# Four gate pairs on seven products, a weave that begins with the key groups, and a new order of the up groups

## The chip, the cores and the metric

The kernel runs on one core of one Trainium2 chip. The metric is the device time of one execution in microseconds (us), and the number that counts is the median of several runs.

## The reference

One layer of a streaming encoder: a feed-forward block, a mixer, a second feed-forward block and a gated input embedding, with a layer norm behind each of the first three. 256 tokens, 2048 channels, all in float32. The change lies in the mixer, whose input `x` is the output of the first norm:

```python
proj = x @ w_in
mq, mk, mv, mo, mi, mf, sq, sk, sv, ga, gb = _split_cols(proj)
qk = jax.nn.silu(_causal_conv(jnp.concatenate([mq, mk], axis=-1), conv_w))
...
h = _mlstm_chunkwise(q, k, v, log_i, log_f)          # 4 heads of 256: the memory half
y_m = head_norm(h) * jax.nn.sigmoid(mo)
y_sb = _stick_breaking(sq, sk, sv)                   # 8 heads of 128: the stick half
merged = jax.nn.sigmoid(ga) * (y_m @ w_up_m) + jax.nn.sigmoid(gb) * (y_sb @ w_up_sb)
return merged @ w_out
```

`ga` and `gb` are 2048 columns each. All other matrix products of the layer have the same form, 256 rows times a weight that is read once from memory.

## The kernel before

**Products of split halves.** A float32 product is made of three faster products. Activations and weights are each split into a rounded high half and the rest as a low half, and TensorE multiplies high by high, high by low and low by high (lines 1462 to 1464) into one PSUM bank. Activations are split once. Each page of a weight (256 rows of 512 columns, 512 KB) is split when it is due: ScalarE casts the high half (line 1388) and VectorE subtracts it to get the low half (line 1392). A `Unit` is the work of one page for one half of the tokens: six matmuls of 512 columns.

**Two ways to do a pair of column groups.** The plain way, `group` (line 410), takes each page for both token halves. So 2048 rows times two groups of 512 columns are 16 pages, 16 splits and 32 units. The other way, `seven` (line 423, called by `both7`), treats the pair as a 2 by 2 block product and forms seven products in place of eight: 28 units for the same pair. It needs sums of weight pages, and each of its 28 units needs a split of its own. Of the sums, some are made by VectorE (line 443) and some by a second load that adds in memory, issued on GpSimd's queue (line 449). `loaded` says which: where it is `every`, two of the four sums of each quad are loads and two are VectorE's. It also needs sums of the activations (`x1T.forms`), made by `forms_later` (line 394): for each of four chunks VectorE does two additions (line 399), four half-width operations (lines 382 to 386) and two subtractions (line 359). When the seven products are there, `both7`'s `done` and `rest` combine them with five VectorE operations and three copies on ScalarE.

**Order.** The whole order of work is written by this program, in one pass. `program` lists units. `weave(main, side)` spreads the side list evenly through the main list. For each unit the pass emits six matmuls, then runs the generators of `Sched` that are due (a clock of 1.297 us per full unit), then emits splits ahead of use until six split pages are held, and then loads ahead of the splits until six (`mix`) or ten (`woven`) unsplit pages are held (`HELD`, line 32). Each engine works through its own queue in that order, so a weight's split stands in VectorE's queue behind every operation that the generators emitted before it. Loads go out on SP's queue in that order too, between the stores of the norm's result, `put_away` (line 331). Such a store waits for an addition that GpSimd's queue issued (line 625), which waits for VectorE's multiplication (line 621).

**The mixer before.** It begins with the plain groups q0, gates, q1, k0 and k1 (lines 1103 to 1107; `conv` at line 868 follows each q or k group with two times six VectorE operations, line 889, behind PE's transposes, line 874). `forms_later` is started after q1. Then comes the weave. Its main list is v0, v1, four stick groups `sb` (the last half as wide), the two plain groups of the first gate pair, `branch(0, 0)` and `branch(0, 1)`, and `ups(0)`, `ups(1)`, `ups(2)`, each a memory half (`w_up_m`, needs `ymT`) followed by a stick half (`w_up_sb`, needs `ysbT`). Its side list is five sevens: stick values, output gates, and gate pairs 1, 2 and 3. After it come `ups(3)` and the output groups. Generators beside it do the four mLSTM heads (`mlstm`, `gated`) and the eight stick heads (`stick`, in lanes). Both chunks of `ymT` (line 1046) are stored to memory when they are ready and brought back before `ups(0)`.

Of the kernel before, what the change touches and what calls it, by code (L numbers as in the profile page):

```python
# [211 lines left out]
        self.name = name  # L212


def weave(main, side):

    n = sum(u.cols for u in main if isinstance(u, Unit))
    out, at, seen = [], 0, 0
    for u in main:
        out.append(u)  # L220
        if isinstance(u, Unit):
            seen += u.cols
            while at < len(side) and at * n < seen * len(side):
                out.append(side[at])
                at += 1
    return out


def flat(pairs):
    return [u for p in pairs for u in p]  # L230
# [7 lines left out]
def kernel(  # L238
# [39 lines left out]
    def big(shape=(P, 1024)):  # L278
        return page_pool.tile(list(shape), F32, name="big", tag="page")
# [114 lines left out]
    def forms_later(act, c):  # L394

        act.whole[c] = big()
        for t in range(TT):
            hi, lo = (act.tiles[c, t][:, k].rearrange("q k s -> q (k s)") for k in range(2))
            nc.vector.tensor_tensor(out=act.whole[c][:, t * COL:(t + 1) * COL], in0=hi, in1=lo, op=ALU.add)
        yield 4.0  # L400
        yield from form_turn(act, c)
# [8 lines left out]
    def group(w, rows, col0, cols, act, done, seed=None):  # L410

        accs = [{} for _ in range(TT)]
        pairs = []
        for i, r in enumerate(rows):
            tile = plain(rows_of(w, r, col0, cols))
            pairs.append([Unit(tile, t, accs[t], act, r // COL, r % COL // P,
                               i == 0, i == len(rows) - 1, done) for t in range(TT)])
            for u in pairs[-1]:
                u.onto = seed is not None
                u.seed = seed if i == 0 else None  # L420
        return pairs
# [436 lines left out]
    def qk_done(which, g):  # L858
        stage = {}

        def done(ps, t):
            stage[t] = temp()
            nc.scalar.copy(stage[t][:], ps)
            if t == TT - 1:
                sched.spawn(conv(which, g, stage), DELAY["cv0"])
        return done
# [85 lines left out]
    def bring_ym_back(units):  # L952

        def one(c, t):
            ymT.tiles[c, t] = act_tile()
            nc.sync.dma_start(out=ymT.tiles[c, t][:].bitcast(F32), in_=ym_rows(c, t))

        out = []
        for i in range(0, len(units), 4):
            out += [lambda i=i: one(i // 8, i // 4 % 2)] + units[i:i + 4] if i < 16 else units[i:i + 4]  # L960
        return out

    def mlstm(h):
        yield from wait("gates", ("qk", 0, h), ("qk", 1, h), ("v", 0, h // 2), ("v", 1, h // 2))
# [55 lines left out]
    def gated(h):  # L1020

        yield from wait(("hs", h), ("mo", 0, h // 2), ("mo", 1, h // 2))
        due = max(sched.now, st.get("gated", 0.0))
        st["gated"] = due + GATED_GAP
        yield due - sched.now
        hs = st["hs", h // 2][:, h % 2]
        for t in range(TT):
            nc.vector.tensor_tensor(out=hs[:, t], in0=hs[:, t], in1=st["mo", t][:, h * DM:(h + 1) * DM], op=ALU.mult)
        yield bank(DELAY["m4"])
        ps = misc([P, TT, 2, P])  # L1030
        parts = []
        for t in range(TT):
            for b in range(2):
                nc.tensor.transpose(ps[:, t, b], hs[:, t, b * P:(b + 1) * P], ident[:])
                k = 2 * (h % 2) + b
                parts.append((ymT.get(h // 2, t)[:, :, k], ps[:, t, b], hs[:, t, b * P:(b + 1) * P],
                              st["cw"][:, 64 + 2 * h + b:65 + 2 * h + b]))
        for _, src, y, g in parts:
            activate(y, src, ACT.Copy, scale=g)
        for d, _, y, _ in parts:  # L1040
            nc.scalar.copy(d[:, 0], y)
            nc.vector.tensor_tensor(out=d[:, 1], in0=y, in1=d[:, 0], op=ALU.subtract)
        for t in range(TT):
            ymT.mark(h // 2, t, 2)
            if ymT.ready(h // 2, t):
                sched.spawn(put_ym_away(h // 2, t), DELAY["away"])

    def stick(h):
# [50 lines left out]
    def in_sequence(gens):  # L1099
        for g in gens:  # L1100
            yield from g
# [1 line left out]
    head = group(w_in, range(0, D, 2 * P), 0, COL, x1T, qk_done(0, 0))  # L1103
    program.extend(skewed(head[:SKEW]) + flat(head[SKEW:]))
    program.extend(flat(group(w_in, range(0, D, 2 * P), 4096, 2 * HM + 2 * DS, x1T, gates_done)))
    for which, g in ((0, 1), (1, 0), (1, 1)):
        program.extend(flat(group(w_in, range(0, D, 2 * P), which * 1024 + g * COL, COL, x1T, qk_done(which, g))))
        if which == 0:
            program.append(lambda: [sched.spawn(forms_later(x1T, c), 4.0 + 12.0 * c) for c in range(4)])
    program.append(lambda: [sched.spawn(in_sequence([mlstm(a), mlstm(a + 1)])) for a in (0, 2)])  # L1110

    def v(g):
        return flat(group(w_in, range(0, D, 2 * P), 2048 + g * COL, COL, x1T, v_done(g)))
# [16 lines left out]
    ga0 = sq0 + 3 * HS * DS  # L1130
    gt = {}

    def gate_done(g, half):
        def done(ps, t):
            if (g, t) not in gt:
                gt[g, t] = big()
            activate(gt[g, t][:, half * COL:(half + 1) * COL], ps, ACT.Sigmoid)
            flags.add(("gate", g, t, half))
        return done

    def merged(g, t):
        return gt[g // 2 * 2, t][:, g % 2 * COL:(g % 2 + 1) * COL]

# [15 lines left out]
            yield 3.0  # L1159
            yield from form_turn(mergedT, g)  # L1160

    def branch(g, half):
        return flat(group(w_in, range(0, D, 2 * P), ga0 + half * D + g * COL, COL, x1T, gate_done(g, half)))

    def ups(g, swap=False):
        parts = [flat(group(w_up_m, range(0, HM * DM, 2 * P), g * COL, COL, ymT, up_done(g, 0, swap))),
                 flat(group(w_up_sb, range(0, HS * DS, 2 * P), g * COL, COL, ysbT, up_done(g, 1, not swap)))]
        if swap:
            parts.reverse()
        return parts[0] + parts[1]  # L1170

    every = (range(4), range(4))

# [9 lines left out]
    def pair(g):  # L1183
        return both7(w_in, ga0 + g * COL, ga0 + D + g * COL, x1T, gate_dest(g), in_two(lambda t: gt[g, t], lambda k, t: ("gate", g, t, k)), every)

    program.append(lambda: [sched.spawn(lane()) for _ in range(2)])
    program.append(lambda: sched.spawn(in_sequence([gated(h) for h in range(HM)])))
    gate = branch(0, 1)
    main = v(0) + v(1) + sb(*SB_GROUPS[0]) + sb(*SB_GROUPS[1]) + [Mode("wide")] + sb(*SB_GROUPS[2]) + sb(*SB_GROUPS[3]) + [lambda: sched.spawn(lane())] + branch(0, 0) + gate[:4] + bring_ym_back(gate[4:] + ups(0)) + ups(1) + ups(2)
    mode("woven")  # L1190
    program.extend(weave(main, in_line([both7(w_in, sq0 + 2 * HS * DS, sq0 + 2 * HS * DS + COL, x1T, sv_dest, sv_ready, later),
                                   both7(w_in, 3072, 3072 + COL, x1T, mo_dest, mo_ready, every), pair(1), pair(2), pair(3)])))
    mode("mix")
    program.append(bring_back)
    program.append(lambda: [sched.spawn(merge_turn(g, t), 1.0 + 2.0 * g + t) for g in range(3) for t in range(TT)])
# [60 lines left out]
    third, fourth = out_group(2), out_group(3)  # L1256
    side = in_line([out7(0, 1)])
    mode("out")
    main = ups(3)
    program.extend(main[:10] + side[:1] + main[10:])  # L1260
    woven = weave(flat(third + fourth[:-SKEW]), side[1:])
    program.extend(woven[:20])
# [257 lines left out]
```

## Time and profile before

| | us |
|---|---|
| median of the three runs | 2152.23 |
| the three runs | 2152.07, 2153.82, 2152.23 |
| the profiled execution | 2151.87 |
| its span, first to last instruction | 2150.2 |

The time of an execution is about 1.7 us more than the span, which lies around it. PE stands for TensorE's matmuls, PEld for its weight loads, DVE for VectorE, ACT for ScalarE, POOL for GpSimd, SP for the queue that issues most transfers. Matmuls are pipelined, so that their recorded durations overlap, and a PE that is busy all the time says little. What tells is the distance from the start of one matmul to the start of the next. The same holds in a small way for VectorE: its operations begin a little before the recorded end of the one before, and the pitch from start to start is what one costs in a full queue. In the mixer the q0 group starts near 688 us, q1 near 725, k0 near 748, k1 near 771, the weave near 794, and `ups(3)` near 1250.

### The profile page before, as it was taken

The page shows a single profiled execution, that of the slowest core. Times are in us where ns is not written, and L with a number is a line of the kernel's source. Part 1 is how long each engine was busy: PE and PEld are TensorE (multiplying, and loading weights), DVE is VectorE, ACT ScalarE, POOL GpSimd, SP SyncE. Part 2 cuts the span into 40 slices and gives each one's busy share as a digit, 9 for nine tenths or more (in the row PEclk, how much of TensorE's full clock was granted, in tenths as well). Part 3 has the DMA queues.
Part 4 walks back from the last instruction along what each step waited for, and adds up shares of the span by engine and source line. Part 5 has one row for each costly group of instructions (what it writes and reads, how often), then busy time and mean ns, then how long its engine had stood idle before and what let it go on. Part 6 is the DMA issues. An engine that isn't in the chain of part 4 may idle for free.

```text
span 2150.2 us, 27845 instructions
## 1 busy us (share of the span) xinstructions
PE 2141.2 (100%) x9742; PEld 1775.6 (83%) x9742; DVE 1866.3 (87%) x2003; ACT 1499.6 (70%) x1946; POOL 160.9 (7%) x190
## 2 busy tenths in 40 slices
PE   9999999999999999999999999999999999999999
PEld 7888888888888888888888887888888888888887
DVE  7899999899987798878888999799998998999773
ACT  6676777777777665678876667757676776776872
POOL 0011000011000000000000000011000011000000
PEclk9999999999999999999999999999999999999999
DMA  9799788998894676868898888788878998889562
GB/s 363 232 264 268 246 262 248 277 266 274 260 313 152 215 263 200 253 208 217 263 280 265 270 234 288 235 224 264 259 248 250 273 280 265 258 261 288 214 181 110
DMA packets 151964, 537.02 MB, mean 250 GB/s; under 512 B 17168, under 2 KB 21776, under 8 KB 151824
## 3 DMA queue, kind: packets, MB, share of 16 engines
q1 hardware_dynamic: 125616, 439.82, 57.1%
q0 software_dynamic: 26208, 95.43, 23.9%
q8 instruction: 76, 1.25, 0.2%
q14 instruction: 64, 0.52, 0.1%
HBM read 528.90 MB, written 6.29 MB: 249 GB/s over the span
## 4 chain that ended last, share of the span: by engine, by line
PE 96%; DVE 2%; DMA 1%; issue 0%; ACT 0%; SPq 0%; DVEq 0%; ACTq 0%
PE mm L1462 31%; PE mm L1464 31%; PE mm L1463 31%; PE ms L363 2%; DVE split L1392 1%; DVE temp L889 0%; DMA raw<-in_ffn_w_dram 0%; DVE raw L443 0%; DMA raw<-in_w_out_dram 0%; PE ms L1086 0%; PE ms L978 0%; PE ms L1056 0%; PE ms L993 0%; ACT split L1388 0%; DVE actT L359 0%
## 5 line engine op out<-in xcount | busy, mean ns | idle before, releaser
L1392 DVE TENSOR_TENSOR split<-raw,split 128x1024 fp32r<-128x1024 f32 (+1 forms) x1102 | 1296.7, 1212 | 158.1 <-ACT split L1388 145.2
L1388 ACT CAST split<-raw 128x1024 fp32r<-128x1024 f32 (+1 forms) x1102 | 1109.2, 1043 | 356.4 <-DVE raw L443 124.9
L1462 PE MATMUL mm<-split,actT 128*128 128x512 f32 x3056 | 1198.4, 392 | 2.1 <-ACT mm L295 2.0
L1464 PE MATMUL mm<-split,actT 128*128 128x512 f32 x3056 | 1185.3, 388 | 0.0
L1463 PE MATMUL mm<-split,actT 128*128 128x512 f32 x3056 | 1184.3, 388 | 0.5 <-DVE split L1392 0.5
L1464 PEld LDWEIGHTS mm<-split,actT 128*128 128x128 f32 x3056 | 574.1, 188 | 118.5 <-DVE actT L359 0.4
L1462 PEld LDWEIGHTS mm<-split,actT 128*128 128x128 f32 x3056 | 574.5, 188 | 116.5 <-ACT mm L295 2.4
L1463 PEld LDWEIGHTS mm<-split,actT 128*128 128x128 f32 x3056 | 574.8, 188 | 114.4 <-DVE split L1392 2.1
L443 DVE TENSOR_TENSOR raw<-raw 128x1024 f32<-128x1024 f32 x214 | 261.3, 1222 | 2.3
L449 POOL DMA_DIRECT2D raw<-in_ffn_w_dram x124 | 108.9, 997 | 1028.6 <-DVE split L1392 859.4
L359 DVE TENSOR_TENSOR actT<-temp,actT 128x512 fp32r<-128x512 f32 (+1 forms) x94 | 62.7, 683 | 47.4 <-ACT actT L358 47.4
L295 ACT ACTIVATE temp<-mm 128x512 f32<-128x512 f32 (+1 forms) x54 | 31.2, 582 | 76.1 <-PE mm L1464 75.8
L717 ACT COPY big<-mm 128x512 f32<-128x512 f32 x80 | 46.8, 585 | 30.4 <-PE mm L1464 30.2
L358 ACT CAST actT<-temp 128x512 fp32r<-128x512 f32 (+1 forms) x94 | 56.9, 616 | 13.0 <-DVE temp L383 7.1
L449 POOL DMA_DIRECT2D raw<-in_w_in_dram x38 | 33.3, 988 | 407.7 <-DVE split L1392 394.9
L724 ACT COPY mm<-big 128x512 f32<-128x512 f32 x96 | 56.4, 590 | 0.0
L371 ACT COPY temp<-ms 128x512 f32<-128x512 f32 x44 | 25.8, 587 | 41.6 <-PE ms L363 40.9
L661 DVE TENSOR_TENSOR temp<-mm,temp 128x512 f32<-128x512 f32 x72 | 49.7, 690 | 5.0 <-PE mm L1464 3.8
L625 POOL DMA_DIRECT2D big<-in_ln_b_dram x12 | 10.4, 864 | 353.1 <-DVE big L621 219.6
L1308 DVE TENSOR_TENSOR temp<-temp,big 128x512 f32<-128x512 f32 (+1 forms) x10 | 5.8, 585 | 32.5 <-ACT temp L295 32.5
L291 ACT ACT_TABLE_LOAD x26 | 33.4, 1283 | 0.5
L359 DVE TENSOR_TENSOR actT<-big,actT 128x512 fp32r<-128x512 f32 x24 | 16.5, 689 | 12.1 <-ACT actT L358 12.1
(140 smaller groups left out, 637.7 us busy)
## 6 DMA issues: line engine op xcount, KB each, us to landing
raw<-in_ffn_w_dram SPq DMA_DIRECT2D x528, 512.0 KB, 6.4
raw<-in_w_in_dram SPq DMA_DIRECT2D x168, 512.0 KB, 5.6
raw<-in_ffn_w_dram POOLq DMA_DIRECT2D x124, 512.0 KB, 8.7
raw<-in_w_in_dram POOLq DMA_DIRECT2D x38, 512.0 KB, 8.9
raw<-in_w_out_dram SPq DMA_DIRECT2D x32, 512.0 KB, 4.7
raw<-in_w_ple_gate_dram SPq DMA_DIRECT2D x32, 512.0 KB, 4.8
raw<-in_w_up_m_dram SPq DMA_DIRECT2D x16, 512.0 KB, 6.2
raw<-in_w_up_sb_dram SPq DMA_DIRECT2D x16, 512.0 KB, 4.8
```

Of the source, the lines that this page charges most:

```text
L358: nc.scalar.copy(hi, ps)
L359: nc.vector.tensor_tensor(out=lo, in0=ps, in1=hi, op=ALU.subtract)
L443: nc.vector.tensor_tensor(out=out.tile[:, :, :cols], in0=a.tile[:, :, :cols], in1=b.tile[:, :, :cols], op=ALU.add)
L449: nc.gpsimd.dma_start(out=whole(out.tile[:]), in_=whole(src), accum_op=ALU.add)
L661: nc.vector.tensor_tensor(out=out, in0=a, in1=b, op=op)
L717: nc.scalar.copy(xres(t, g * COL), ps)
L724: nc.scalar.copy(ps, xres(t, g * COL))
L1388: nc.scalar.copy(hi[:, ks], r[:, ks])
L1392: nc.vector.tensor_tensor(out=lo[:, ks], in0=r[:, ks], in1=hi[:, ks], op=ALU.subtract)
L1462: nc.tensor.matmul(ps, hi, w[0][:, k, :u.cols], start=first, stop=False, skip_group_check=u.onto)
L1463: nc.tensor.matmul(ps, hi, w[1][:, k, :u.cols], start=False, stop=False, skip_group_check=u.onto)
L1464: nc.tensor.matmul(ps, lo, w[0][:, k, :u.cols], start=False, stop=last, skip_group_check=u.onto)
```

## The change

All four gate pairs go through `both7`, so `branch` and `gate_done` are gone and the side list has six sevens. The k groups and v groups move into the weave's main list, in a new order. `weave` gets a lead of 8 full units: nine units of the side follow the first unit of the main list, one follows each unit after that, and the last eight units of the main list have none beside them. `forms_later` starts one group earlier, with delays of 1, 13, 25 and 37 in place of 4, 16, 28 and 40. mLSTM heads 0 and 1 run first, then 2 and 3, so only the first chunk of `ymT` is stored and brought back, now around the last stick group. Of the up groups 0 to 2 all three memory halves come first, then all three stick halves.

```diff
-def weave(main, side):
+def weave(main, side, lead=0):
...
-    out, at, seen = [], 0, 0
+    out, at, seen = [], 0, lead * COL
...
-        out = []
-        for i in range(0, len(units), 4):
-            out += [lambda i=i: one(i // 8, i // 4 % 2)] + units[i:i + 4] if i < 16 else units[i:i + 4]
-        return out
+        return [lambda: one(0, 0)] + units[:4] + [lambda: one(0, 1)] + units[4:]
...
-            if ymT.ready(h // 2, t):
+            if h < 2 and ymT.ready(h // 2, t):
...
-    for which, g in ((0, 1), (1, 0), (1, 1)):
-        program.extend(flat(group(w_in, range(0, D, 2 * P), which * 1024 + g * COL, COL, x1T, qk_done(which, g))))
-        if which == 0:
-            program.append(lambda: [sched.spawn(forms_later(x1T, c), 4.0 + 12.0 * c) for c in range(4)])
-    program.append(lambda: [sched.spawn(in_sequence([mlstm(a), mlstm(a + 1)])) for a in (0, 2)])
+    def qk(which, g):
+        return flat(group(w_in, range(0, D, 2 * P), which * 1024 + g * COL, COL, x1T, qk_done(which, g)))
+
+    program.append(lambda: [sched.spawn(forms_later(x1T, c), 1.0 + 12.0 * c) for c in range(4)])
+    program.extend(qk(0, 1))
...
-    def branch(g, half):
-        return flat(group(w_in, range(0, D, 2 * P), ga0 + half * D + g * COL, COL, x1T, gate_done(g, half)))
-
-    def ups(g, swap=False):
...
+    def up_m(g):
+        return flat(group(w_up_m, range(0, HM * DM, 2 * P), g * COL, COL, ymT, up_done(g, 0, False)))
+
+    def up_sb(g):
+        return flat(group(w_up_sb, range(0, HS * DS, 2 * P), g * COL, COL, ysbT, up_done(g, 1, True)))
...
+    program.append(lambda: [sched.spawn(in_sequence([mlstm(a), mlstm(a + 2)])) for a in (0, 1)])
...
-    gate = branch(0, 1)
-    main = v(0) + v(1) + sb(*SB_GROUPS[0]) + sb(*SB_GROUPS[1]) + [Mode("wide")] + sb(*SB_GROUPS[2]) + sb(*SB_GROUPS[3]) + [lambda: sched.spawn(lane())] + branch(0, 0) + gate[:4] + bring_ym_back(gate[4:] + ups(0)) + ups(1) + ups(2)
+    sbs = [sb(*heads) for heads in SB_GROUPS]
+    main = qk(1, 0) + v(0) + sbs[0] + sbs[1] + qk(1, 1) + v(1) + [Mode("wide")] + sbs[2] + bring_ym_back(sbs[3]) + [lambda: sched.spawn(lane())]
+    main += up_m(0) + up_m(1) + up_m(2) + up_sb(0) + up_sb(1) + up_sb(2)
...
-                                   both7(w_in, 3072, 3072 + COL, x1T, mo_dest, mo_ready, every), pair(1), pair(2), pair(3)])))
+                                   both7(w_in, 3072, 3072 + COL, x1T, mo_dest, mo_ready, every)] + [pair(g) for g in range(4)]), 8))
...
-    main = ups(3)
+    main = up_m(3) + up_sb(3)
```

More of the change, by code (lines that the diff above doesn't have):

```diff
@@ L1131 @@
     gt = {}
[L1133 to L1139, printed above, removed]
     def merged(g, t):
@@ L1160, in merge_turn @@
             yield from form_turn(mergedT, g)
-    def branch(g, half):
-        return flat(group(w_in, range(0, D, 2 * P), ga0 + half * D + g * COL, COL, x1T, gate_done(g, half)))
-    def ups(g, swap=False):
[L1166 to L1170, printed above, removed]
+    def up_m(g):
+        return flat(group(w_up_m, range(0, HM * DM, 2 * P), g * COL, COL, ymT, up_done(g, 0, False)))
+    def up_sb(g):
+        return flat(group(w_up_sb, range(0, HS * DS, 2 * P), g * COL, COL, ysbT, up_done(g, 1, True)))
     every = (range(4), range(4))
```

## The prediction

> **What bounds the kernel now.** I read the page first, then the chain of waits in order of time, then the windows over the mixer, and at last VectorE's and SP's timelines at the place where the change cuts in.
>
> ```profile
> span 2150.2 us, 27845 instructions
> ...
> PE 2141.2 (100%) x9742; PEld 1775.6 (83%) x9742; DVE 1866.3 (87%) x2003; ACT 1499.6 (70%) x1946; POOL 160.9 (7%) x190
> ...
> PE 96%; DVE 2%; DMA 1%; issue 0%; ACT 0%; SPq 0%; DVEq 0%; ACTq 0%
> ```
>
> PE carries 96% of the chain that ended last: the time is PE's work, and PE loses very little to waits. What a unit costs PE stands in its timeline, at the place where q1 ends and k0 begins:
>
> ```profile
> 747.70 0.39 PE L1462 MATMUL mm<-split,actT 128*128 128x512 f32 x1
> ...
> 749.06 0.60 PE L874 MATMUL ms<-ident,temp 128*128 128x128 f32 x4
> 749.42 0.47 PE L1462 MATMUL mm<-split,actT 128*128 128x512 f32 x1
> ```
>
> The first unit of k0 lasts from 747.70 to 749.06: **1.36 us a unit**. Four transposes of q1's convolution follow, and cost 0.44 us (0.36 until the next matmul starts, and 0.08 by which that one is longer). The 2% that the chain gives to DVE are worth more than their share, since most of them lie in one place, where the mixer begins:
>
> ```profile
> 771.64 1.06 ACT split L1388
> 772.72 1.23 DVE split L1392
> ...
> 812.87 1.15 DVE split L1392
> 814.06 0.50 PE mm L1463
> ```
>
> From 772 to 814 the chain runs through VectorE alone, with the convolutions, the sums of activations and the splits. At 814.06 one piece of PE lasts 0.50 us, where its neighbours last 0.23: PE waited 0.27 us. So in this stretch VectorE had spent every page that it was ahead, and was just in time. The windows give its load:
>
> ```profile
> 724.90:747.00 22.10, 22.10 (x103) 18.10 (x102) 19.38 (x27) 12.46 (x21) 1.75 (x3) 1.00 0.73 218
> 747.70:814.00 66.30, 66.30 (x306) 54.44 (x304) 61.02 (x96) 44.41 (x61) 2.62 (x3) 1.00 0.77 251
> 747.70:1250.00 502.30, 502.14 (x2320) 416.52 (x2319) 427.25 (x529) 352.48 (x499) 34.17 (x39) 1.00 0.81 248
> 1330.00:1340.00 10.00, 8.04 (x36) 6.34 (x35) 9.97 (x11) 6.91 (x9) 0.00 (x0) 1.00 0.74 244
> ```
>
> The columns behind the length are PE, PEld, DVE, ACT, POOL, clock, DMA share and GB/s. Over the mixer DVE is busy 427.25 of 502.30 us (85%), in the stretch up to 814 it is 61.02 of 66.30 (92%). The last row is PE's only other loss of size here: 1.96 us, in the output groups.
>
> **The change part by part.** *Pair 0 on seven products:* 28 units in place of 32, 4 x 1.36 = **5.4 us of PE saved**. It costs the other engines. A split and a sum of weights, and the operations that combine products, are these rows:
>
> ```profile
> L1392 DVE TENSOR_TENSOR split<-raw,split 128x1024 fp32r<-128x1024 f32 x23 | 27.5, 1220 | 4.5 <-ACT split L1388 4.5
> L443 DVE TENSOR_TENSOR raw<-raw 128x1024 f32<-128x1024 f32 x3 | 3.6, 1219 | 0.0
> ...
> L509 DVE TENSOR_TENSOR big<-mm,big 128x512 f32<-128x512 f32 x15 | 10.3, 688 | 1.6 <-PE mm L1464 1.3
> ```
>
> 28 splits in place of 16, 8 sums (two per quad on VectorE) and five combining operations: 12 + 8 operations of 1.22 and 5 of 0.69 make 28 us of DVE by recorded durations. ACT gets 12 casts of about 1.04 and some copies, 14 us on an engine that was idle for 150 us of the 502. Spread over the weave both are hidden under PE: (427 + 28) / 497 is 92%, and the stretch up to 814 ran at 92% with a loss of 0.27 us. What matters is where it is crowded.
>
> *The weave's start with q1, a lead of 8, forms earlier.* Here I count VectorE's queue against PE's time. What one costs in a full queue is its pitch:
>
> ```profile
> 750.61 2.94 DVE L889 SCALAR_TENSOR_TENSOR temp<-ms,cw,temp 128x253 f32<-128x253 f32 x6
> 753.46 1.22 DVE L1392 TENSOR_TENSOR split<-raw,split 128x1024 fp32r<-128x1024 f32 x1
> 754.59 0.69 DVE L621 TENSOR_TENSOR big<-big 128x512 f32<-128x512 f32 x1
> 755.19 1.29 DVE L399 TENSOR_TENSOR big<-actT 128x512 f32<-128x512 f32 x2
> 756.39 0.17 DVE L852 COPY aT<-ms 128x8 f32<-128x8 f32 x1
> ...
> 762.62 0.42 DVE L382 TENSOR_TENSOR temp<-big 128x256 f32<-128x256 f32 x1
> ...
> 764.08 2.36 DVE L1392 TENSOR_TENSOR split<-raw,split 128x1024 fp32r<-128x1024 f32 x2
> 766.35 1.29 DVE L359 TENSOR_TENSOR actT<-temp,actT 128x512 fp32r<-128x512 f32 x2
> ```
>
> Half a convolution takes 2.85 us (750.61 to 753.46), two splits 2.27, so one 1.135, and a sum of weights as much, since it lasts as long. The forms of one chunk take 1.20 + 1.46 + 1.20 = 3.86 (755.19 to 756.39, 762.62 to 764.08, and for the two of L359, which last as long as the two of L399, the same 1.20).
>
> The order of the new weave, by its formula: one unit of k0, nine units of the side, then one of each in turn. The 17th page of the side (the first of its last quad's four middle products) is then PE's 26th unit, due 25 x 1.36 + 2 x 0.44 = 34.9 us behind 747.7, at 782.6. From the start of q1, at 724.9, that is 57.7 us. In VectorE's queue ahead of that page stand:
>
> - 19.4 us that are there already by 747 (window row), five pages of splits ahead included;
> - the forms of all four chunks, 4 x 3.86 = 15.4 (before, none was started ahead of 747);
> - q1's convolution 5.7, and L621 with L852 0.7;
> - five sums for the first three quads of stick values, 5.7 (three of them for the first quad, whose sums are all VectorE's at that point);
> - 22 pages, less the five ahead: 17 x 1.135 = 19.3.
>
> Together 66.2 us, **8.5 us more than PE's 57.7**. The same count over the second window row, before the change, gives 23 splits, three sums, six half convolutions, four forms and 0.7: 62.7, where the row has 61.02 busy. So it is a little high, and I take 8.0. The pages ahead don't cover it: they are already counted as done. The idle time of DVE before 747 isn't free either; there it is 2.7 us of 22.1 and counted as used up. Walking the queue in order, the waits fall ahead of the sixth to the tenth page of the side, where a half convolution or a form stands between two splits, from about 754 to 772. Afterwards the pair of one main and one side unit costs PE 2.72 us and DVE some 2.1 (1.5 splits, 0.29 sums, 0.1 combining), and DVE gets ahead again. Bounds: 0, if 8.5 us of the forms and the convolution stood behind that page in the queue and not ahead of it, and 11, if operations cost what they last. I take 8.0, because the count before came out within 3%.
>
> [...] The rows above have the next operation start 0.08 us ahead of the recorded end, so the pitch stands.
>
> *What goes:* the wait of 0.27 us at 814, as the convolution of k1 comes far later. *The order of up groups, the mLSTM pairs, `ymT`:* the same instructions, less two stores and two loads of 512 KB. They cost nothing as long as the heads are ready:
>
> ```profile
> L968 PE MATMUL ms<-big x8: 374/426/479, 834.5 to 920.2; 4*128 4x256 f32 x8
> ...
> L1086 PE MATMUL ms<-temp,big x32: 271/326/426, 984.9 to 1134.7; 128*128 128x256 f32 x16, 128*128 128x128 f32 x16
> ```
>
> mLSTM heads start 85.7 / 3 = 29 us apart when they queue. Heads 2 and 3 need v1, which ends 200 units into the weave, near 1043 with 23 us for small matmuls and the wait. Even one after another, with 20 for the gated turns, they are ready near 1121. `up_m(0)` asks for them 256 units in, near 1127. Eight stick heads end 150 / 7 = 21 us apart; the last two can start near 1116 and are due near 1199. If that cover fails, PE waits for what is missing, a few us. The end of the weave, eight main units alone, asks less of DVE; the loss at 1330 lies 80 us behind it, and I leave it as it is.
>
> **Sum** on the profiled execution (2151.87 us, 1.7 more than its span): 2151.87 - 5.4 + 8.0 - 0.3 = 2154.2. The median of the runs is 0.36 above that execution: **2154.5**.
>
> **The rivals.** *A, VectorE keeps up.* If the early pages are made in gaps that my count takes for full, only the saving stays: 2152.2 - 5.4 - 0.3 = 2146.5, and 2145 if the quiet end of the weave shortens the 1.96 us. For it: DVE at 85% over the whole mixer. Against it: 61.02 of 66.30 before the side was there, and PE already waiting. [...]
>
> *B, SP's queue stands behind the stores.*
>
> ```profile
> 754.23 0.33 SPq L331 DMA_DIRECT2D away<-big  x1
> 754.65 2.20 SPq L1365 DMA_DIRECT2D raw<-in_w_in_dram  x4
> 765.16 0.33 SPq L331 DMA_DIRECT2D away<-big  x1
> ...
> 755.81 0.87 POOL L625 DMA_DIRECT2D big<-in_ln_b_dram  x1 [10.92 <-issue]
> ```
>
> Between 756.9 and 765.2 SP issues no load: the fourth store waits for GpSimd's addition (755.81), which waits for the multiplication at 754.59. With 12 plain pages ahead that was harmless. In the new order that multiplication stands in the late queue, some 8 us later, so loads behind the store go out near 773 and land 5.6 us or more later (the page's median for SP), near 779 to 783. By the order of the loads, the weave's 13th to 15th pages go out behind that store, and are due near 783. From a store later than about 771 it decides, and adds what it is late, 3 to 6 us: 2157.5 to 2160.5. For it: the long waits seen here. Against it: ten pages held, not six.
>
> *C, DVE stays late.* At 92% it may pay again where the next convolutions, the last sums of a pair and its combining operations fall together, 1 to 3 us more, 2156 to 2158. That the change does less than it says can't be: the four units are gone by count.
>
> **How the numbers follow.** The forecast has 0.45, by itself 2151.5 to 2157.5 (waits of 5 to 11 us). A has 0.27, B 0.16, C 0.12. The measurement of this kernel can tell about 0.2%, 4.3 us. Faster than 2147.9 is A: 0.27. Slower than 2156.5 are B, half of C and the forecast's upper end: 0.16 + 0.06 + 0.05 = 0.27. The rest is 0.46. The range takes in A without its lowest and B without its highest values: 2146 to 2160.
>
> **What would show it.** Right: waits of PE for splits of 5 us or more in sum between 750 and 785, with DVE busy without a gap there, the chain in DVE, and from 850 on a PE as full as before. The weave's end, less its start, is then about 3 us longer, and the stretch from there to the end unchanged. Wrong: a PE without waits there (A), waits that end with a DMA (B), or losses in the up groups.

## The result: 1.5% slower, and most of it where nothing was expected

The changed kernel takes **2184.17 us** (median, 2183.09 to 2186.05), the kernel before 2152.34 us in the same runs. The ratio is 1.0147, with a 95% interval of 1.0134 to 1.0159: some 32 us slower. The forecast was 2154.5 us with a range of 2146 to 2160. So the direction of its early loss was right and its total wrong by 30 us.

Lines have moved, and after the change the matmuls are L1449 to L1451 (L1462 to L1464 before), ScalarE's cast is L1375 (L1388), VectorE's split L1379 (L1392), SP's load L1352 (L1365), and the sticks' matmuls are L1071 to L1073 and L1083. Lines up to 957 are the same.

The page of the changed kernel has these lines for the ones shown of before:

```profile
span 2181.4 us, 27900 instructions
...
PE 2146.1 (98%) x9718; PEld 1771.6 (81%) x9718; DVE 1891.8 (87%) x2028; ACT 1522.4 (70%) x1967; POOL 168.0 (8%) x198
...
PE 43%; DVE 1%; DMA 0%; issue 0%; ACT 0%; DVEq 0%
```

The 24 matmuls are gone (9742 to 9718), and the span is 31.2 us longer. The chain of waits that ended last covers only the last 44% of the span and shows almost nothing of the mixer, so the waits have to be read stretch by stretch. First, where the loss lies. The first transpose of the merges behind the weave (L363) is the same point of the program in both kernels. These are its rows, of the kernel before and then of the changed one:

```profile
L363 PE MATMUL ms<-ident,big x32: 270/273/273, 1251.8 to 1292.1; 128*128 128x128 f32 x32
```

```profile
L363 PE MATMUL ms<-ident,big x24: 272/273/273, 1284.3 to 1292.3; 128*128 128x128 f32 x24
```

It starts at 1251.8 before and at 1284.3 after, 32.5 us later; from there to the end of the span are 898.4 us and 897.1. The first unit of k0 starts at 747.70 before and at 747.30 after. So the whole loss lies between these two points, in the weave. Its windows, changed kernel (columns as in the prediction):

```profile
724.90:747.00 22.10, 22.10 (x102) 18.05 (x102) 21.10 (x33) 11.90 (x18) 1.29 (x2) 1.00 0.84 258
747.00:793.80 46.80, 39.29 (x168) 30.32 (x166) 46.29 (x64) 32.26 (x41) 6.56 (x8) 0.96 0.95 260
...
963.00:1041.00 78.00, 73.28 (x322) 60.27 (x322) 63.00 (x78) 58.35 (x81) 7.00 (x8) 0.96 0.74 222
...
1100.00:1250.00 150.00, 134.91 (x645) 109.31 (x644) 118.52 (x149) 105.11 (x153) 10.53 (x12) 1.00 0.74 216
```

Length less PE is what PE stood idle: 7.5 us up to 794, 4.7 between 963 and 1041, **15.1 between 1100 and 1250**; the two stretches left out hold 0.6. In the kernel before, the view of waits has no row for PE between 747 and 1250, and its late stretch reads:

```profile
1100.00:1250.00 150.00, 149.89 (x666) 123.97 (x665) 131.36 (x133) 93.72 (x108) 8.75 (x10) 1.00 0.87 272
```

In the first stretch VectorE is busy for 46.29 of 46.80 us. In the last it is idle for 31 of 150, and does less than before (118.52 us against 131.36): whatever makes PE wait there, it is not the amount of VectorE's work. What PE waited for, between 747 and 1250 (the view of waits: in total, times, longest):

```profile
PE ms L874 <- ACT temp L863: 5.7, 2, 3.8
PE ms L1083 <- DVE temp L889: 2.9, 1, 2.9
PE ms L1083 <- DVE temp L1074: 2.7, 1, 2.7
PE ms L1072 <- DVE actT L1068: 2.6, 2, 1.7
PE mm L1450 <- DVE split L1379: 2.4, 4, 0.9
PE ms L1031 <- DVE big L1025: 2.4, 2, 1.2
```

Only 2.4 us are waits for splits. Most end at a small matmul (`ms`) of a convolution, a head or a stick, whose operand ScalarE or VectorE made late.

**The early wait.** It is one of 3.8 us, and three engines' timelines show how it comes about. VectorE, then ScalarE, then PE, changed kernel:

```profile
745.08 1.21 DVE L1379 TENSOR_TENSOR split<-raw,split 128x1024 fp32r<-128x1024 f32 x1
746.21 1.27 DVE L399 TENSOR_TENSOR big<-actT 128x512 f32<-128x512 f32 x2
747.42 0.67 DVE L621 TENSOR_TENSOR big<-big 128x512 f32<-128x512 f32 x1
748.02 1.21 DVE L1379 TENSOR_TENSOR split<-raw,split 128x1024 fp32r<-128x1024 f32 x1
749.16 0.67 DVE L621 TENSOR_TENSOR big<-big 128x512 f32<-128x512 f32 x1
749.76 2.34 DVE L443 TENSOR_TENSOR raw<-raw 128x1024 f32<-128x1024 f32 x2
```

```profile
745.18 1.05 ACT L1375 CAST split<-raw 128x1024 fp32r<-128x1024 f32 x1 [5.07 <-DVE raw L443]
751.04 1.04 ACT L1375 CAST split<-raw 128x1024 fp32r<-128x1024 f32 x1 [4.81 <-DVE raw L443]
751.99 1.07 ACT L863 COPY temp<-mm 128x512 f32<-128x512 f32 x2
```

```profile
748.43 0.39 PE L1451 MATMUL mm<-split,actT 128*128 128x512 f32 x1
752.62 1.39 PE L874 MATMUL ms<-ident,temp 128*128 128x128 f32 x4 [3.80 <-ACT temp L863]
```

PE starts q1's last matmul at 747.07 and then does the first unit of k0, whose last matmul is the one at 748.43. Next in its queue are the transposes of q1. For these ScalarE must copy q1 out of PSUM (L863). In ScalarE's queue the copy stands behind a cast, the cast needs a sum of weight pages (L443), and the sum stands in VectorE's queue, which has no gap. So ScalarE sits idle for 4.81 us up to 751.04, then does the cast, and the copy starts at 751.99, 4.9 us behind the start of q1's last matmul.

**The late waits.** There are sixteen between 1108 and 1215. This is one of them, in the same three timelines:

```profile
1153.25 1.23 DVE L1379 TENSOR_TENSOR split<-raw,split 128x1024 fp32r<-128x1024 f32 x1 [2.37 <-PE mm L1450]
```

```profile
1154.51 1.99 ACT L1375 CAST split<-raw 128x1024 fp32r<-128x1024 f32 x2 [3.00 <-DVE split L1379]
1156.41 0.36 ACT L806 COPY big<-ms 128x256 f32<-128x256 f32 x1
```

```profile
1156.82 0.44 PE L1071 MATMUL ms<-actT,tri 128*128 128x384 f32 x1 [2.08 <-ACT big L806]
```

Here VectorE is idle, for 2.37 us, until a matmul ends. A split reads two pages that no matmul writes, so the only matmul it has to wait for is the last reader of the page tile that it is to write into. There are 51 such tiles (`PAGES`, line 26), shared by loaded pages, split pages and the larger results. This is read from the program; the profile doesn't count tiles, and wide10 below tests it. Behind that split ScalarE's next cast waits 3.00 us, and behind the cast stands the copy of a head's transpose (L806). PE's next matmul is a stick's (L1071), and the profile puts its wait of 2.08 us down to L806. Over 1100 to 1250 these waits of VectorE add up; changed kernel, then before:

```profile
DVE split L1379 <- PE mm L1450: 9.3, 7, 2.4
```

```profile
DVE split L1392 <- PE mm L1463: 1.7, 2, 1.3
```

### The profile page after: what moved, and what is told of

It is laid out like the page before. It is cut to its first block, busy times and chain, and to the rows that moved or that the text cites. A ratio compares the mean times of both kernels' runs of the same rounds, so it can differ in the third digit from the quotient of the medians.

```text
span 2181.4 us, 27900 instructions
## 1 busy us (share of the span) xinstructions
PE 2146.1 (98%) x9718; PEld 1771.6 (81%) x9718; DVE 1891.8 (87%) x2028; ACT 1522.4 (70%) x1967; POOL 168.0 (8%) x198
## 5 line engine op out<-in xcount | busy, mean ns | idle before, releaser
L1379 DVE TENSOR_TENSOR split<-raw,split 128x1024 fp32r<-128x1024 f32 (+1 forms) x1114 | 1310.1, 1210 | 168.0 <-ACT split L1375 141.7
L1375 ACT CAST split<-raw 128x1024 fp32r<-128x1024 f32 (+1 forms) x1114 | 1122.2, 1043 | 397.2 <-DVE raw L443 136.9
L1449 PE MATMUL mm<-split,actT 128*128 128x512 f32 (+1 forms) x3048 | 1195.7, 392 | 1.7 <-ACT mm L295 0.9
L1450 PE MATMUL mm<-split,actT 128*128 128x512 f32 (+1 forms) x3048 | 1181.8, 388 | 2.9 <-DVE split L1379 2.9
L1451 PE MATMUL mm<-split,actT 128*128 128x512 f32 (+1 forms) x3048 | 1182.3, 388 | 1.3 <-DVE actT L359 1.3
L1451 PEld LDWEIGHTS mm<-split,actT 128*128 128x128 f32 x3048 | 573.2, 188 | 120.7 <-DVE actT L359 2.2
L1449 PEld LDWEIGHTS mm<-split,actT 128*128 128x128 f32 x3048 | 573.7, 188 | 116.2 <-ACT mm L295 1.3
L443 DVE TENSOR_TENSOR raw<-raw 128x1024 f32<-128x1024 f32 x222 | 270.5, 1220 | 2.5
L295 ACT ACTIVATE temp<-mm 128x512 f32<-128x512 f32 (+1 forms) x54 | 31.2, 583 | 76.4 <-PE mm L1451 76.0
L449 POOL DMA_DIRECT2D raw<-in_w_in_dram x46 | 40.6, 996 | 429.9 <-DVE split L1379 359.3
L625 POOL DMA_DIRECT2D big<-in_ln_b_dram x12 | 10.4, 866 | 351.2 <-DVE big L621 227.1
```

Source lines behind the costliest of these rows:

```text
L443: nc.vector.tensor_tensor(out=out.tile[:, :, :cols], in0=a.tile[:, :, :cols], in1=b.tile[:, :, :cols], op=ALU.add)
L449: nc.gpsimd.dma_start(out=whole(out.tile[:]), in_=whole(src), accum_op=ALU.add)
L1375: nc.scalar.copy(hi[:, ks], r[:, ks])
L1379: nc.vector.tensor_tensor(out=lo[:, ks], in0=r[:, ks], in1=hi[:, ks], op=ALU.subtract)
L1449: nc.tensor.matmul(ps, hi, w[0][:, k, :u.cols], start=first, stop=False, skip_group_check=u.onto)
L1450: nc.tensor.matmul(ps, hi, w[1][:, k, :u.cols], start=False, stop=False, skip_group_check=u.onto)
```

## The experiments

Three theories go in. **D**: the early loss is the amount of VectorE's work between about 725 and 795, wherever it comes to light. **S** (at first a part of D, later its rival): it is ScalarE's copy out of PSUM (the texts call it an evacuation) in the queue behind a cast, with too little slack. **P**: the late loss is page tiles that are not free in time. The texts that follow also name **B** (here, other than rival B of the prediction: the small products of the second halves are bunched) and, near the end, **W** (the denser weave). The gaps quoted are PE's, over 0.15 us. A ratio is to the kernel before, with its 95% interval.

**The burst: lead0**

```diff
-    ... [pair(g) for g in range(4)]), 8))
+    ... [pair(g) for g in range(4)]), 0))
```

> The changed kernel with no lead: its weave still begins at k0, but one side unit follows each main unit, not nine the first. Changed kernel: PE idle 7.5 us between 747 and 794, 4.7 between 963 and 1041, 15 between 1100 and 1250. Theory D (the burst of nine units with its sums, beside convolution and forms, makes VectorE's queue late, and evacuations wait behind it): the first loss falls from 7.5 us to under 3, the later ones stay; time about 2176. Theory P (page tiles run out in the second half of the weave): as D for the later losses, since the lead moves the same pages by eight units only. Theory B (the small products of the second halves are bunched): as P.

2185.2 us, 1.0146 [1.0117, 1.0175]. The early gaps are 5.6 us in place of 7.5, where D gave under 3, and the later ones are as before or moved. The nine side units in a row are not the main cause; VectorE's queue is as full without them (46.34 of 46.80 us up to 794).

**The sums by loads: sv_loads**

```diff
-    ... x1T, sv_dest, sv_ready, later),
+    ... x1T, sv_dest, sv_ready, every),
```

> The changed kernel, but the first quad of the stick values has two of its four weight sums made by adding loads and not by VectorE. Theory D in the form that a cast on ScalarE waits for VectorE's sum and holds back the evacuation behind it: the wait of 3.8 us at 748 goes to under 1, the idle time of PE between 747 and 794 from 7.5 to about 3.5; later stretches as in the changed kernel; time about 2178. If only VectorE's amount of work counts, the two sums are 2.3 us less, and 7.5 goes to about 5. If loads are what is late there, it grows.

2185.84 us, 1.0149 [1.012, 1.0178]. VectorE is busy for 43.62 us up to 794, 2.7 less, and PE waits all the same: the casts ahead of q1's copy now wait for loads (11.0 us in three such waits, the longest 7.4), and the early gaps are 7.6 us. Both forms of D, with 3.5 and 5 us, missed: the wait has another last cause, so less work for VectorE is not enough where loads take its place.

**Fewer pages held: wide10; the groups in the old order: order_old; both: order_wide**

```diff
-HELD = {..., "wide": (12, 6), ...}
+HELD = {..., "wide": (10, 6), ...}
```

```diff
-    main = qk(1, 0) + v(0) + sbs[0] + sbs[1] + qk(1, 1) + v(1) + ...
+    main = qk(1, 0) + qk(1, 1) + v(0) + v(1) + sbs[0] + sbs[1] + ...
```

> The changed kernel with at most 10 in place of 12 loaded pages held in the second half of the weave (the mode called wide), which leaves two pages more to the splits. Theory P: PE's idle time between 1100 and 1250 falls from 15 us to under 5, VectorE's waits for PE there from 9.3 us to under 3; the stretch up to 1041 as before; time about 2170. Theory B, and the theory that VectorE has too much work there: idle time stays at 13 to 16 us, time 2182 to 2186.

> The changed kernel with its main list in the order k0, k1, v0, v1 and then the stick groups, so that convolutions and mLSTM heads come early and not in the second half. Theory B: the losses between 963 and 1041 and from 1100 to 1250 (4.7 and 15 us of idle PE) fall by more than half; time about 2168. Theory P: the loss of 963 to 1041, where no page is short, moves with the convolution of k1, and that from 1100 on stays, since as many pages are held there; time 2178 to 2186.

> The changed kernel with both edits of the two that gained: at most 10 loaded pages held in the second half of the weave, and the main list in the order k0, k1, v0, v1, stick groups. If they take away different losses (order: 4.7 us idle between 963 and 1041; pages: some 10 us from 1100 on), they add up: 2184 - 12 - 12 = 2160, with the early loss of 7 us and some 3 us from 1100 on left. If both only relieve the pages of the second half, together they give no more than one: 2170.

wide10 takes 2172.95 us, 1.0089 [1.006, 1.0118]; order_old 2171.93, 1.0084 [1.0055, 1.0114], which neither P (2178 to 2186) nor B (about 2168) gave; both together **2160.48, 1.0034 [1.002, 1.0047]**. Windows of the late stretch in wide10, of the stretch of k1's convolution in order_old, and of both in order_wide:

```profile
1100.00:1250.00 150.00, 145.42 (x700) 120.21 (x700) 128.92 (x161) 111.43 (x161) 10.53 (x12) 1.00 0.80 242
```

```profile
963.00:1041.00 78.00, 77.99 (x360) 64.56 (x359) 67.74 (x98) 61.99 (x103) 7.02 (x8) 1.00 0.82 255
```

```profile
747.00:793.80 46.80, 39.91 (x168) 30.74 (x167) 46.29 (x64) 31.63 (x40) 6.99 (x8) 0.96 0.97 260
...
963.00:1041.00 78.00, 77.99 (x361) 64.53 (x360) 67.85 (x98) 61.73 (x103) 7.02 (x8) 1.00 0.84 254
...
1100.00:1250.00 150.00, 146.61 (x709) 122.46 (x708) 130.12 (x150) 108.54 (x150) 8.80 (x10) 1.00 0.83 258
```

With two unsplit pages fewer held, PE's idle time in the late stretch falls from 15.1 to 4.6 us, and VectorE's wait for a matmul ahead of a split from 9.3 to 0.9: P holds for two thirds of that stretch. From 1000 us to the end of the weave VectorE's and ScalarE's operations stand in the same order in wide10 and in the changed kernel, but for a handful of splits a few places apart, so it is not their order that helped; nor does a wait of these two or of PE over 0.6 us end with a load in the late stretch of the changed kernel. With the old order, too, two pages fewer bring 7.6 us (11.0 of idle time in order_old, 3.4 in order_wide). But there VectorE waits for a matmul ahead of a split for only 0.8 us; ScalarE's casts, which need a free tile as well, wait for matmuls for 30.6 us and then 16.6. Which of the two engines passes the lateness on in that order was not shown. With k1 back ahead of the sticks, the 4.7 us between 963 and 1041 are gone; there a stick's matmul (L1083) had waited 2.9 us behind k1's taps (L889) in VectorE's queue, and k1's transposes 1.9. The two edits nearly add up: by medians they bring 11.2 and 12.2 us alone and 23.7 together, and measured from the kernel before in the same runs 12.6, 13.6 and 24.0. What is left is the early stretch, 7.3 us, much as in the changed kernel.

**Is it the amount? forms_early, forms_early8** (order_wide, and the forms started ahead of the gates group, 12 and 8 us apart)

```diff
+    program.append(lambda: [sched.spawn(forms_later(x1T, c), 1.0 + 12.0 * c) for c in range(4)])
     program.extend(flat(group(w_in, range(0, D, 2 * P), 4096, 2 * HM + 2 * DS, x1T, gates_done)))
...
-    program.append(lambda: [sched.spawn(forms_later(x1T, c), 1.0 + 12.0 * c) for c in range(4)])
     program.extend(qk(0, 1))
```

> As the run with both edits, and the sums of activations started one group earlier still, behind q0, with the same 12 us between chunks. The same instructions; some 8 us of VectorE's work move from behind 747 to the gates group, where it idles 3.7 us of 13.7. Theory D (too much of VectorE's queue at the weave's start): the early loss falls from 7 us to 2 to 4, and the wait of 3.8 us for the evacuation of q1 at 748 to under 2; time 4 to 6 us below that run. If what is late there is the loads behind the stores on SP's queue, nothing changes.

> As the last, with 8 us between chunks, so that all four chunks are issued by 745. Theory D: the early loss falls further if VectorE still has room ahead of 747, to 1 to 3 us; if the queue is then late already in q1, the wait at 748 grows and the gain over the last is none.

2160.71 us, 1.0041 [1.0025, 1.0057], and 2164.47, 1.0051 [1.0028, 1.0074]. Nothing is gained by doing the forms earlier, and D's 4 to 6 us are missed. The room that they were to use was not used: in the gates group (711.2 to 724.9) VectorE idles 3.9 us of 13.7 in forms_early and 3.7 in order_wide. The lateness gathers in the one wait ahead of q1's transposes, 7.6 us and 11.8. That the time stays the same is also what the text gives for late loads. Against that speaks that VectorE, for whose sums most of the waiting casts wait, is itself busy for 46.24 us of 46.80 up to 794.

**More slack for the transposes: cv_late** (order_wide, with the convolution's transposes due later)

```diff
-    "cv0": 1.0,
+    "cv0": 6.0,
```

> The kernel with both edits (old order of the main list, ten pages in the wide mode; 2160.48 us, 7.3 us of waits between 748 and 794 and 1.7 us of half clock), and here the transposes of a q or k group's convolution are due 6.0 us behind its last unit in place of 1.0. Theory S (what is lost early is lost because ScalarE's evacuation of q1 stands in its queue behind a cast that waits for VectorE's weight sum, and the transposes that wait for it have 1 us of slack, while the splits have 8): the wait of 3.8 us ahead of the transposes at 749 goes, and with it the half clock of 1.7, the split waits of 3.5 us stay: about 2155. Theory D (the amount of VectorE's work between 725 and 795 is what counts, so the lateness comes out somewhere): the same 7 us, now ahead of matmuls that wait for splits, and 2160.

2163.9 us, 1.0051 [1.0036, 1.0066]. The waits of order_wide and of cv_late:

```profile
PE ms L874 <- ACT temp L863: 4.0, 2, 3.8
PE mm L1450 <- DVE split L1379: 2.2, 3, 1.0
```

```profile
PE mm L1450 <- DVE split L1379: 7.1, 7, 3.5
PE mm L1451 <- DVE actT L359: 1.7, 1, 1.7
```

The wait at the transposes is gone, and the time comes back ahead of matmuls that wait mostly for splits: 6.6 us between 752 and 772, and 2.4 more at 789 and 797. It is more than D's 7 us, and the mean granted clock between 747 and 794 is 0.93 in place of 0.96, by an estimate about two stretches of 3.4 us at half clock in place of one. S falls: ScalarE's queue decides where the lateness shows, but giving it slack takes none away.

**Less work: no_taps** (order_wide; leaves out the twelve VectorE taps of q1's convolution)

```diff
-                for j in range(3):
+                for j in range(0 if (which, g) == (0, 1) else 3):
```

> The kernel with both edits, and the convolution of q1 leaves out its three earlier taps, that is the twelve VectorE operations of about 0.5 us each (6 us of VectorE; ScalarE's product with the last tap stays). So the output is another. Theory D (amount of VectorE's work): the early loss falls by what comes behind the convolution in VectorE's queue, from 7.3 to about 2 to 4 us, with the first wait of 3.8 us unchanged, as the convolution stands behind it: 2156 to 2158. Theory S (ScalarE's queue and slack alone): only what waits for the convolution itself changes, 0 to 1 us: 2159.5 to 2160.5.

2156.96 us, 1.0017 [1.0008, 1.0026]: 3.5 us less than order_wide for 6 us of VectorE's work taken out. PE's waits:

```profile
PE ms L874 <- ACT temp L863: 4.0, 2, 3.8
PE mm L1450 <- DVE split L1379: 0.9, 1, 0.9
...
PE mm L1451 <- DVE actT L359: 0.7, 1, 0.7
```

What stood ahead of the taps is unchanged (4.0), and what stood behind them has shrunk (2.2 to 0.9, 1.3 to 0.7, and ScalarE's 0.8 at 769 is gone). The early loss is 4.7 us, a little over D's 2 to 4, and the time is as D gave it. So VectorE's work is a cause of the early loss, by place in the queue too; but of the 6 us taken out only 3.5 came back.

**Thinning it out with the taps in: cv_l2_f16, cv_l0_f16_w11** (cv_late; a lead of 2 or 0, forms at 1, 17, 33, 49; the second with 11 pages in the wide mode)

> The kernel with both edits and the late transposes, and two further ways to thin out VectorE's early queue: the lead of the side is 2 in place of 8 and the forms' delays are 1, 17, 33 and 49. Theory D: some 5 to 8 us of splits, sums and forms move from ahead of 790 to behind it, where VectorE has room (it is idle for 15 of 78 us between 963 and 1041 in the changed kernel), and the early loss falls to 0 to 2 us: about 2152 to 2154. Theory S: nothing beyond what the late transposes brought.

> As the one before, with a lead of 0 and eleven pages in the wide mode (with ten it doesn't come out). Theory D: early loss 0 to 1 us, but the denser end of the weave has fewer free pages, 1 to 4 us more between 1100 and 1250: 2152 to 2157. Theory S: nothing beyond what the late transposes brought, and the same late loss.

2162.99 us, 1.0048 [1.0032, 1.0065], and 2165.2, 1.0057 [1.0042, 1.0072]. A miss for theory D's numbers: the waits go on, now up to 803 and 824. The early gaps are some 8 us in the first and 6.7 in the second: the stretch stays full, it only becomes longer.

**The weave where it was, with the fourth pair on seven: k_ahead_w12, ka_11_11_4, ka_10_11_4** (both key groups ahead of the weave, forms behind q1, a lead of 4; 12 pages held, or 11, or 10 and then 11; the first held 12 in both parts of the weave, not 10 in the second as its text says)

```diff
     program.extend(qk(0, 1))
+    program.append(lambda: [sched.spawn(forms_later(x1T, c), 4.0 + 12.0 * c) for c in range(4)])
+    program.extend(qk(1, 0))
+    program.extend(qk(1, 1))
...
-    main = qk(1, 0) + v(0) + sbs[0] + sbs[1] + qk(1, 1) + v(1) + ...
+    main = v(0) + v(1) + sbs[0] + sbs[1] + ...
```

> The old start: k0 and k1 ahead of the weave with the sums of activations behind q1 as before the change, then the weave with all six sevens beside a shorter main list (v0, v1, stick and up groups), a lead of 4, at most 12 loaded pages in the first half of the weave (it needs them) and 10 in the second. Theory D: no loss of PE between 747 and 794; the first loss, of some 11 us with the slower clock behind it, is gone. But the weave is denser, 168 side units beside 136: VectorE gets 79% from the two lists alone before any small product, so later losses grow. Theory P: with 12 pages held they grow from the first half on. Time 2155 to 2175.

> The kernel with both key groups ahead of the weave and the fourth gate pair kept on seven products (with twelve pages in both modes 2167.16 us, 3.2 us of waits between 794 and 816 and 10.4 between 1100 and 1200), here with eleven pages held in both modes. Theory P (the late waits come from page tiles that are not free in time): they fall to some 4 to 6 us, 2160 to 2163. Theory W (they come from the denser weave: 168 units of the side beside 136 of the main list, so that the sticks' and heads' small products get less of VectorE and ScalarE between them): they stay near 10 us, 2166 to 2168.

> As the one before, with ten pages in the first part of the weave and eleven in the wide mode. Theory P: within 1.5 us of the one before, since the late stretch lies in the wide mode; theory W: near 10 us of late waits, 2166 to 2168. Should fewer pages ahead cost something in the first part, it would be waits that end with a DMA there; none is expected.

2167.16 us, 1.007 [1.0047, 1.0093]; 2163.55, 1.0049 [1.0032, 1.0066]; 2163.86, 1.0047 [1.0032, 1.0062]. The early loss is down to 3.4 us, at 795 to 815, where the side begins. The late one is 10.4, 8.1 and 8.5 us. That lies between P (4 to 6) and W (near 10); by time the last two are close to P's 2160 to 2163 and below W's 2166 to 2168, and they lie 0.3 us apart, within P's 1.5. So neither is shown to be the whole cause: the sticks' small products still wait, the longest for 3.0 us (L1053 for VectorE's L1074). The fourth pair doesn't pay there either.

**A group without a convolution ahead of the weave: v0_ahead, v0_thin** (order_wide; q1 and v0 change places; the second also with a lead of 2 and the forms at 6, 20, 34, 48)

```diff
-    program.extend(qk(0, 1))
+    program.extend(v(0))
...
-    main = qk(1, 0) + qk(1, 1) + v(0) + v(1) + sbs[0] + sbs[1] + ...
+    main = qk(1, 0) + qk(0, 1) + qk(1, 1) + v(1) + sbs[0] + sbs[1] + ...
```

> The kernel with both edits, and q1 and v0 change places: v0, which has no convolution, is the plain group ahead of the weave, and q1 stands behind k0 in the weave's main list. So 5.7 us of VectorE's work leave the crowded stretch and come some 45 us later, where VectorE is not full; nothing is left out. Theory D (amount of VectorE's work between 725 and 795): as without the taps, and the wait ahead of the transposes at 749 goes too, as there are none: early loss 2 to 4 us in place of 7.3, the rest as in the kernel with both edits: 2154 to 2157. If the lateness is carried on instead until the convolutions of k0 and q1 come: waits near 800 to 830, and 2158 to 2161.

> As the one before, with a lead of 2 in place of 8 and the forms' delays at 6, 20, 34 and 48. Without the convolution there is room for the work that these two move behind 795: theory D gives an early loss of 0 to 2 us and 2152 to 2155. If the lateness is only carried on: waits between 800 and 830 as with q1 ahead, and 2157 to 2161.

2161.22 us, 1.0034 [1.0022, 1.0045], above D's range and at the upper end of the other one, with 5.2 us idle up to 794 and a wait of 2.0 us at 830, and **2157.43, 1.0019 [1.001, 1.0028]**, the best of the versions that leave nothing out, but again in the range of lateness carried on and not in D's. v0_thin's early windows:

```profile
724.90:747.00 22.10, 22.10 (x104) 18.09 (x103) 20.94 (x32) 12.34 (x21) 1.63 (x4) 1.00 0.83 262
747.00:793.80 46.80, 44.76 (x197) 35.88 (x195) 46.35 (x57) 29.68 (x38) 6.39 (x8) 1.00 1.01 296
```

VectorE is as full as ever (46.35 of 46.80), but with splits rather than taps, and PE loses 2.0 us there, 1.7 up to 820, and some 4 more by waits of up to 1.4 us between 1100 and 1200, most at heads and sticks. None of the versions beats the kernel before.

Taken together, VectorE's full queue is where the early loss comes from, and no_taps shows that less work in it helps. D as a rule for how much didn't hold: work moved to another time mostly brought its lateness along, in forms_early, in cv_l2_f16 and cv_l0_f16_w11, and in v0_ahead and v0_thin.

## Why the prediction was wrong, point by point

- *4 units of 1.36 us saved.* Right by count: 24 matmuls fewer.
- *VectorE is 8.0 us late at the start of the weave.* Right engine, and near in size: 7.5 us of idle PE, with VectorE busy for 46.29 of 46.80 us, or some 9 with the stretch at half clock behind it. How much of the agreement is luck is open, since a convolution of 5.7 us left out of the same queue brought only 3.5 back. The pitch in a full queue is as counted: the split of 745.08 costs 1.13 us to the next start at 746.21. Rival A, "VectorE keeps up", has fallen.
- *The waits fall ahead of the sixth to the tenth page, 754 to 772.* Wrong in place: half of it, 3.8 us, came at 749 at q1's transposes, and the waits for splits up to 794, forecast as 5 us or more, are 1.6 us. The count looked at splits alone, which have six pages of slack; ScalarE's copy has about one unit. cv_late gave the transposes that slack, and most of the waits then fell between 752 and 772, as forecast, but they did not become smaller.
- *"Walking the queue … DVE gets ahead again", "from 850 on a PE as full as before".* **This step failed.** VectorE did get ahead (118.52 of 150 us busy late in the weave), and PE lost 15.1 us all the same. The working asked whether there was time for the work, and never whether there was room for it: with the sevens of four pairs beside the up groups, splits wait until a matmul has read the page tile that they are to write into, and the small products behind them wait in the same queues. Holding two pages fewer brought 10.5 of the 15.1 us back, and the old order on top of that 1.2 more. The last 3.4 us stay open, and so does which tiles fill the pool.
- *"The order of up groups, the mLSTM pairs, ymT … cost nothing as long as the heads are ready."* The heads were ready; no up group waited for one. But the change also put k1 behind two stick groups, and the text gave that no cost. Its convolution stood in VectorE's queue ahead of sticks: 4.7 us idle, all of it gone in order_old. This term, put at nothing, is the second step that failed.
- *The transfers (rival B).* Not seen: none of PE's waits in the weave ends with a DMA. Where a cast waits for a load (3.6 us in two waits up to 800), VectorE still has work in its queue. The store in question went out at 769.56 us, 4.4 later than before, not 8, and ahead of the 771 from which it was to decide.
- *Rival C* had 1 to 3 us for "late again later"; it was 20.4 us idle after 794. Its mechanism, the next convolution in a full queue, fits the 4.7 us at k1 and not the 15.1 behind 1100.

The sum, with what was measured: -5.4 for the four units, +7.5 early, +4.7 at k1, +15.1 late, +0.6 elsewhere, +5.1 for three spans at half clock (3 x 1.7, an estimate; last section), 27.6 us of the 32.9 by which the weave is longer (537.0 us from k0's first unit to L363, 504.1 before). Most of the other 5.3 us is how idle time is counted, by an estimate: it starts at the recorded end of a matmul, 0.39 us behind its start, while in a full queue the next one starts 0.23 behind. So each of the 24 waits costs 0.16 us more than its row says, 3.8 us in all. The rest was not separated.

## What to carry to other kernels

Before more work is woven beside a stretch, count two things: the time of each engine in queue order, and the tiles that are held at once. Idle time of an engine said nothing here: VectorE was idle for 31 of 150 us late in the weave, where its splits waited 9.3 us for matmuls, and PE lost 15.1 us. And the lateness of one full engine (46.29 of 46.80 us busy) came out first at the waiter with the least slack, a small copy on another engine, with a wait of 3.8 us. Moving that waiter moved the loss (cv_late), and moving the work mostly did too; leaving work out made the loss smaller (7.3 us to 4.7 in no_taps).

## What the runs showed of the hardware

Some waits of PE cost more here than their length. In the mixer of the changed kernel three of them stand beside a stretch at half the granted clock. The windows at the first show 0.57 in 4 us, that is 3.4 us at a half:

```profile
748.00:752.00 4.00, 0.82 (x4) 0.36 (x2) 4.00 (x5) 0.96 (x2) 1.75 (x2) 1.00 0.85 184
752.00:756.00 4.00, 3.37 (x10) 2.64 (x11) 3.95 (x8) 3.89 (x8) 0.00 (x0) 0.57 1.06 210
756.00:760.00 4.00, 4.00 (x21) 3.08 (x20) 3.86 (x8) 3.98 (x5) 0.00 (x0) 1.00 1.02 275
```

In the stretch at 752.42 matmuls start 0.43 us apart (754.24, 754.67, 755.09) and behind it 0.23, so about half the work is done, and each such stretch costs about 1.7 us, by an estimate from these numbers. The three begin at 752.42, 1008.42 and 1025.49 and last 3.4 us each (the windows from 1008 to 1012 and from 1025 to 1029 show 0.57 too); the waits beside them are of 3.80, 1.87 and 2.85 us and end at 752.62, 1008.24 and 1024.66. Other waits of such a length have no such stretch. The changed kernel has one of 2.08 us that ends at 1156.82 and one of 2.72 us that ends at 1214.80, and the kernel before one of 1.96 us that ends at 1333.83:

```profile
1154.00:1158.00 4.00, 1.92 (x11) 1.37 (x10) 2.89 (x4) 2.26 (x3) 0.00 (x0) 1.00 0.41 131
1211.00:1215.00 4.00, 1.28 (x6) 0.79 (x5) 3.13 (x4) 2.61 (x3) 0.00 (x0) 1.00 1.04 221
1215.00:1219.00 4.00, 4.00 (x20) 3.33 (x20) 1.63 (x3) 1.66 (x4) 0.00 (x0) 1.00 0.77 249
```

The clock is 1.00 in these windows, and before the change it is 1.00 between 1330 and 1340. So the length of a wait alone doesn't tell whether such a stretch comes with it, since 1.87 us had one and 2.72 us had none; what decides it was not shown. In forms_early8, with the wait of 11.8 us, the mean clock between 747 and 794 is 0.85, by an estimate some 14 us at a half; in order_wide, with 3.8 us as the longest, it is 0.96.
